# Moving adaLN modulation sums between TensorE and VectorE, and earlier in the program, in a hybrid gMLP / linear-attention layer

## The chip, the cores and the metric

One core of one Trainium2 chip runs the whole layer. The metric is the device time of one execution in microseconds; the median of several runs is given. The kernel is bound by its matrix products, which are all split into three products of 32-bit parts (a high part rounded to fp32r and the rest as a low part: high x high, high x low, low x high).

## The reference

One trunk layer with x (512 tokens, width 2048) and a context (256 tokens). Only x is returned. Six vectors per stream, `mod = silu(c) @ w_mod + b_mod`, modulate the normalised rows; for the context the vector is `c_ctx` and only the first two of the six are needed.

```python
mod_x = split((silu(c) @ w_mod + b_mod), 6);  mod_c = split(silu(c_ctx) @ w_mod + b_mod, 6)
hx = rms_norm(x, g_pre_mix) * (1 + mod_x[1]) + mod_x[0]
hc = rms_norm(xc, g_pre_mix) * (1 + mod_c[1]) + mod_c[0]
ux, vx, qx, kx, vvx, gx, dfx, dbx = split_proj(hx @ w_in)      # the context's likewise, from hc
a_x = spatial_gating(gelu(ux), layer_norm(gelu(vx)))           # gMLP heads
gla_x = bidir_gla(x's q, k, v, decays; states that start from the context's)
x = x + mod_x[2] * rms_norm(concat(a_x, gla_out(gla_x, gx)) @ w_out, g_post_mix)
h2 = rms_norm(x, g_pre_ffn) * (1 + mod_x[4]) + mod_x[3]
x = x + mod_x[5] * rms_norm((silu(h2 @ w1) * (h2 @ w2)) @ w_ffn_out, g_post_ffn)
```

## The kernel before

Activations are held transposed: 16 tiles `hx[k]` of 128 features by 512 tokens for x, 16 tiles `hc[k]` for the context. A tile k of hx needs the modulation of its 128 features, a column of `modA` (gain times 1 + scale) and one of `modB` (shift). `modulated(k)` (L396) turns the tile on TensorE, applies A and B on ScalarE, and makes the high part (ScalarE) and the low part (VectorE).

There are two ways to make the columns. `mod_both(k0)` (L429) makes two tiles for x and context at once on TensorE: the 16 row blocks of `w_mod` are the moving operand, the two conditioning vectors the stationary one, 16 matmuls into two rows of one PSUM bank; then the bias is added on VectorE (L447), eight tiny matmuls (L450) turn the rows into columns, and four VectorE instructions write A and B of both. `mod_ab` (L247) makes nk tiles for one of the two: `mod_acc` (L212) sums over the 16 row blocks on VectorE, one fused multiply-add (L228) of 128 x (2 nk 128) per block, and `mod_ab` then sums over the partitions with 2 nk matmuls of one column each (L257) and writes A and B with two small VectorE instructions (L260, L261). `mod_acc` has a parameter `lag`: how many loads are asked ahead of the multiply-add; `late` in `mod_ab` puts generator steps between the last multiply-add and the column sums.

The order. Everything is issued by one Python program; a list scheduler behind it orders each engine's queue by program order and by when it thinks an operand is ready. Background work is written as generators. In the first products of x (L506 to L542) the loop runs over three groups of tiles, 0 to 3, 4 to 7 and 8 to 15. In each group it does x's keys, the last query head and the decay's low rank together ("k loop", 17 products per tile), then three query heads ("q loop", 9 per tile), then the first half of gMLP's u ("u loop", 12 per tile). After each tile `mods_ahead(2)` takes two steps of the generator `mods_x` (L458): first tiles 2 and 3 by `mod_both(2)`, then x's tiles 4 to 7, 8 to 11 and 12 to 15 by `mod_ab`. Five steps are taken before the loop (L503). `mods_until` forces the steps that a tile needs. Its loads use a pool of ten raw buffers of 512 KB and two accumulators (L419), closed after the u loop of the last group (L543); the context's rows are loaded into the room that it leaves (L570).

Then come the blocks u1, v0 and v1 of the gMLP (16 weight tiles each), the context's keys and values ck and cv, and the linear attention's vv0, vv1, g0, g1. Behind them run two pumps, `bg` and `bgm`, stepped at a rate per weight tile. `bgm` carries the modulation: `ctx_mod` (L550) makes the context's tiles (columns for tiles 4 to 15 in three `mod_ab`, tiles 0 to 3 having come with `mod_both`), at 1.3 steps per weight tile, and is drained after v1 (L662). Then `mods_ffn_in` (L665), the modulation of the FFN norm, at 0.6 in ck and cv and 0.85 in the linear attention (L953), drained at L997. Loads of background sums go to SP's queue by `load_behind` (L198), behind the latest weight load.

Of the kernel before, what the change touches and what calls it, by code (L numbers as in the profile page):

```python
# [18 lines left out]
P = 128  # L19
D = 2048  # L20
KT = D // P
# [71 lines left out]
def trunk_kernel(ctx, tc, cmat, cmask, x, c, ctxt, c_ctx, w_mod, b_mod, g_pre_mix, g_post_mix, g_pre_ffn,  # L93
# [4 lines left out]
    bg, bgm = Pump(), Pump()  # L98
# [11 lines left out]
    def bank(name, main=True):  # L110
        return pm.tile([P, 512], F32, tag="mm" if main else "ms", bufs=6 if main else 2, name=name)
# [4 lines left out]
    def mm(o, l, r, start, stop):  # L116
        return T.matmul(o, lhsT=l, rhs=r, start=start, stop=stop)  # L117
# [20 lines left out]
    cx, cc = cpair[:, :KT], cpair[:, KT:]  # L138
    gpm, gpf, outg, lng = (vec[:, a:b] for a, b in ((0, 16), (16, 32), (32, 40), (40, 48)))
# [54 lines left out]
    def load(dst, src):  # L194

        latest[0] = nc.sync.dma_start(dst, src).ins
# [9 lines left out]
    def mod_pool(pool, nraw, nacc, fetch):  # L206
        return (lambda n: pool.tile([P, 1024], F32, tag="rawm", bufs=nraw, name=n),
                lambda n: pool.tile([P, 1024], F32, tag="macc", bufs=nacc, name=n), fetch)

    mod_bg = mod_pool(stg, 3, 1, load_behind)  # L210
# [33 lines left out]
            yield None  # L244
        yield acc

    def mod_ab(base, k0, nk, cvec, gv, A, B, name, tiles, pin=False, late=0):  # L247

        n = f"{name}{k0}"
        for acc in mod_acc(base + k0 * P, nk * P, 2, cvec, n, tiles, pin):  # L250
            if acc is None:
                yield
        for _ in range(late):
            yield
        ps = bank(n + "ps", False)
        for j in range(2 * nk):
            ins = mm(ps[:, j:j + 1], acc[:, j * P:(j + 1) * P], ones[:, 0:1], True, True)  # L257
            if late and j == 0:
                tc.keep_in_program_order(ins)
        V.tensor_copy(B[:, k0:k0 + nk], ps[:, 0:nk])  # L260
        V.scalar_tensor_tensor(out=A[:, k0:k0 + nk], in0=ps[:, nk:2 * nk], scalar=1.0, in1=gv[:, k0:k0 + nk],  # L261
                               op0=ALU.add, op1=ALU.mult)
        yield
# [99 lines left out]
    cmodA = cp.tile([P, KT], F32, name="cmodA")  # L363
    cmodB = cp.tile([P, KT], F32, name="cmodB")
    fmodA = cp.tile([P, KT], F32, name="fmodA")
    fmodB = cp.tile([P, KT], F32, name="fmodB")
# [52 lines left out]
    mod_first = mod_pool(sp, 10, 2, load_behind)  # L419
# [9 lines left out]
    def mod_both(k0):  # L429

        n = f"mb{k0}"
        ps = bank(n + "ps", False)
        brow = slot(n + "b")[0:2, :]
        for i in range(2):
            nc.scalar.dma_start(brow[:, i * 256:(i + 1) * 256],
                                b_mod[0:1, i * D + k0 * P:i * D + k0 * P + 256].to_broadcast([2, 256]))
        for r0 in range(0, KT, 2):
            raw = mod_first[0](f"{n}w{r0}").rearrange("p (k i c) -> p k i c", k=2, i=2)
            for j in range(2):
                r = r0 + j  # L440
                (load if k0 == 0 else load_behind)(
                    raw[:, j], w_mod[0, r * P:(r + 1) * P, 0:2 * D].rearrange("r (i c) -> r i c", i=2)[
                        :, :, k0 * P:k0 * P + 256])
                mm(ps[0:2, :], cpair[:, r:r + KT + 1:KT], raw[:, j].rearrange("p i c -> p (i c)"), r == 0, r == KT - 1)
            yield
        row = slot(n + "r")[0:2, :]
        V.tensor_tensor(out=row, in0=ps[0:2, :], in1=brow, op=ALU.add)  # L447
        pc = bank(n + "pc", False)
        for j in range(4):
            mm(pc[:, 2 * j:2 * j + 2], row[0:2, j * P:(j + 1) * P], ident[0:2, 0:2], True, True)  # L450
        q = pc[:, 0:8].rearrange("p (i k j) -> p i k j", i=2, k=2)
        k2 = slice(k0, k0 + 2)
        for j, A, B in ((0, modA, modB), (1, cmodA, cmodB)):
            V.tensor_copy(B[:, k2], q[:, 0, :, j])
            V.scalar_tensor_tensor(out=A[:, k2], in0=q[:, 1, :, j], scalar=1.0, in1=gpm[:, k2], op0=ALU.add,
                                   op1=ALU.mult)

    def mods_x():  # L458
        yield from mod_both(2)
        ready[0] = 4  # L460
        yield
        for k0, nk in ((4, 4), (8, 4), (12, 4)):
            yield from mod_ab(0, k0, nk, cx, gpm, modA, modB, "mx", mod_first, k0 == 2)
            ready[0] = k0 + nk
            yield

    ready = [2]
    mx = mods_x()

    def mods_until(k):  # L470
# [3 lines left out]
    def mods_ahead(n):  # L474
        for _ in range(n):
            next(mx, None)
# [23 lines left out]

    for k in range(2):
        first_weights(k)
    mods_ahead(5)  # L503

    upart = [slot(f"up{b}") for b in range(4)]
    for ka, kb in ((0, 4), (4, 8), (8, KT)):  # L506
        first, last = ka == 0, kb == KT
        acc_k = [bank(f"k{h}") for h in range(HB)]
        acc_q = bank("q3")
        acc_d = bank("d")  # L510
        for k in range(ka, kb):
            mods_until(k + 1)
            modulate_until(k + 2)
            first_weights(k)
            wq, wk = w0.pop(k)
            st, sp_ = k == ka, k == kb - 1
            for h in range(HB):
                three(acc_k[h], cut(wk, h * P, P), hx[k], st, sp_)
            three(acc_q, cut(wq, 0, P), hx[k], st, sp_)
            low_rank(acc_d[:64, :], wd[k], hx[k], st, sp_)  # L520
            mods_ahead(2 if k > 1 else 2)
        for h in range(HB):
            land(acc_k[h], kq[h][:, 0, :], first)
        land(acc_q, kq[3][:, 1, :], first, QSCALE)
        land(acc_d, dT[:64, :], first, 1.0, 64)
        accs = [bank(f"q{h}") for h in range(3)]
        for k, (w,) in stream(w_in[0], OQ, 384, kb - ka, f"wq{ka}", k_first=ka):
            for h in range(3):
                three(accs[h], cut(w, h * P, P), hx[ka + k], k == 0, k == kb - ka - 1)
            mods_ahead(2)  # L530
        for h in range(3):
            land(accs[h], kq[h][:, 1, :], first, QSCALE)
        accs = [bank(f"u0{b}") for b in range(4)]
        for k, (w,) in stream(w_in[0], OU, 512, kb - ka, f"wu{ka}", k_first=ka):
            for b in range(4):
                three(accs[b], cut(w, b * P, P), hx[ka + k], k == 0, k == kb - ka - 1)
            mods_ahead(2)
        for b in range(4):
            land(accs[b], upart[b], first)
            if last:  # L540
                S.activation(upart[b], upart[b], AF.Gelu_apprx_tanh)
                nc.scalar.dma_start(u_dr[b], upart[b])  # L542
    sp_ctx.close()  # L543


# [2 lines left out]
    hc = [None] * KT  # L548

    def ctx_mod():  # L550
        for k0 in range(0, KT, 4):
            if k0:
                yield from mod_ab(0, k0, 4, cc, gpm, cmodA, cmodB, "mc", mod_bg, late=2)
            for kb in (k0 // 2, k0 // 2 + 1):
                ps = bank(f"xcp{kb}", False)
                f = slot(f"xcT{kb}")
                for j in range(2):
                    k = 2 * kb + j
                    c = slice(j * CTX, (j + 1) * CTX)
                    turn(ps[:, c], xcn, k)  # L560
                    S.activation(f[:, c], ps[:, c], AF.Identity, bias=cmodB[:, k:k + 1], scale=cmodA[:, k:k + 1])
                hi = hcp.tile([P, 512], F32R, name=f"hch{kb}")
                lo = hcp.tile([P, 512], F32R, name=f"hcl{kb}")
                S.copy(hi, f)
                V.tensor_tensor(out=lo, in0=f, in1=hi.bitcast(F32), op=ALU.subtract)
                for j in range(2):
                    hc[2 * kb + j] = cut((hi, lo), j * CTX, CTX)
                yield

    xcn = [[hcp.tile([P, 512], F32, name=f"xc{t}_{b}") for b in range(4)] for t in range(NC)]  # L570
    for t in range(NC):
        load_rows(xcn[t], ctxt, t)
    normalise(xcn, "xc")[1]()
    bgm.add(ctx_mod())
    bg.rate, bgm.rate = 0.75, 1.3

    def block_ws(w, c0, nb, name, hook=None):
# [77 lines left out]
    for g in range(2):  # L655
# [3 lines left out]
            S.activation(ev, ps, AF.Gelu_apprx_tanh)  # L659
            vt.append(ev)  # L660
        bg.add(gating(g, vt))
    bgm.drain()  # L662


    def mods_ffn_in():  # L665
        for k0 in range(0, KT, 4):
            yield from mod_ab(3 * D, k0, 4, cx, gpf, fmodA, fmodB, "mf", mod_bg, late=1)

    bgm.add(mods_ffn_in())
    bgm.rate = 0.6  # L670
    ckT = [slot(f"ckT{i}") for i in range(2)]
    ckt = [slot(f"ckt{t}") for t in range(NC)]
    cacc = [bank(f"ck{t}") for t in range(NC)]
# [40 lines left out]
    for o in (0, 512):  # L714
        n = min(512, len(LEVELS) * P - o)
        mf = slot(f"mf{o}")
# [233 lines left out]
        bg.add(ctx_state(h))  # L950
    for h in range(HB):
        bg.add(gla_scores(h), 1)
    bg.rate, bgm.rate = 2.4, 0.85  # L953
    for g in range(2):
        for t, ps in enumerate(block_as(w_in[0], OVV + g * 512, f"vv{g}")):
            S.copy(vv[t][g], ps)
# [473 lines left out]
```

## Time and profile before

| | before |
|---|---|
| median of 3 runs | 2330.3 us (2327.45 to 2330.81) |
| the profiled execution | 2326.27 us |
| its span, first to last instruction | 2324.5 us |
| mean granted TensorE clock | 0.99 |
| TensorE / VectorE / ScalarE busy | 97% / 69% / 42% of the span |
| bytes moved | 483.58 MB |

Busy time of TensorE is from the start of one matmul to its modelled end; neighbours overlap, so the pitch of equal matmuls is read from a stretch with their count. The granted clock is 1.00 at 2.4 GHz and 0.50 at 1.2 GHz. The idle time in brackets behind an instruction is that of its engine just before it, and what ended it.

### The profile page before, as it was taken

The page shows a single profiled execution, that of the slowest core. Times are in us where ns is not written, and L with a number is a line of the kernel's source. Part 1 is how long each engine was busy: PE and PEld are TensorE (multiplying, and loading weights), DVE is VectorE, ACT ScalarE, POOL GpSimd, SP SyncE. Part 2 cuts the span into 40 slices and gives each one's busy share as a digit, 9 for nine tenths or more (in the row PEclk, how much of TensorE's full clock was granted, in tenths as well). Part 3 has the DMA queues.
Part 4 walks back from the last instruction along what each step waited for, and adds up shares of the span by engine and source line. Part 5 has one row for each costly group of instructions (what it writes and reads, how often), then busy time and mean ns, then how long its engine had stood idle before and what let it go on. Part 6 is the DMA issues. An engine that isn't in the chain of part 4 may idle for free.

```text
span 2324.5 us, 27744 instructions
## 1 busy us (share of the span) xinstructions
PE 2258.6 (97%) x10298; PEld 1833.0 (79%) x10298; DVE 1599.9 (69%) x2072; ACT 987.6 (42%) x1517; POOL 15.5 (1%) x24
## 2 busy tenths in 40 slices
PE   7999999999999999999999999999999999999998
PEld 2778887788888887777778888888888788888886
DVE  3886587677795656788877877787788643354346
ACT  4444334465565326753333444444445322231232
POOL 0000000000000000000000000000000000000000
PEclk9999999999999999999999999999999999999999
DMA  9966788854452777767776665766575654474344
GB/s 319 329 225 227 246 293 282 274 164 130 152 188 87 261 250 239 231 215 225 235 245 190 217 193 179 226 208 190 177 232 191 221 192 152 133 229 165 120 137 154
DMA packets 255403, 483.58 MB, mean 208 GB/s; under 512 B 21482, under 2 KB 32962, under 8 KB 255268
## 3 DMA queue, kind: packets, MB, share of 16 engines
q1 hardware_dynamic: 243392, 461.98, 61.4%
q10 hardware_dynamic: 11876, 19.84, 2.4%
q8 instruction: 80, 1.31, 0.2%
q14 instruction: 55, 0.45, 0.1%
HBM read 455.52 MB, written 26.22 MB: 207 GB/s over the span
## 4 chain that ended last, share of the span: by engine, by line
PE 82%; DMA 8%; DVE 6%; ACT 2%; issue 1%; SPq 0%; DVEq 0%; ACTq 0%
PE fo L117 16%; PE wo L117 4%; PE f9p L117 3%; PE f5p L117 3%; PE f6p L117 3%; PE f7p L117 3%; PE f8p L117 3%; PE f4p L117 3%; PE f3p L117 3%; PE f10p L117 3%; PE f1p L117 3%; PE f2p L117 2%; PE vv1a L117 2%; PE v0a L117 2%; PE u1a L117 2%; PE k L117 2%
## 5 line engine op out<-in xcount | busy, mean ns | idle before, releaser
L1239 DVE TENSOR_TENSOR gl<-gr,gh 128x512 fp32r<-128x512 f32 x44 | 29.1, 687 | 26.3 <-ACT gh L1238 26.2
L1238 ACT CAST gh<-gr 128x512 fp32r<-128x512 f32 x44 | 25.4, 618 | 48.2 <-DMA gr<-g_dr 41.3
L228 DVE SCALAR_TENSOR_TENSOR m21acc<-m21w,cpair,m21acc 128x1024 f32<-128x1024 f32 x16 | 20.5, 1283 | 15.8 <-DMA m21w<-in_w_mod_dram 15.6
L228 DVE SCALAR_TENSOR_TENSOR m53acc<-m53w,cpair,m53acc 128x512 f32<-128x512 f32 x16 | 12.0, 751 | 27.5 <-DMA m53w<-in_w_mod_dram 27.5
L856 ACT ACTIVATE lv<-lv 128x1024 f32<-128x1024 f32 x20 | 21.0, 1056 | 21.8 <-DVE lv L855 21.8
L117 PE MATMUL fo<-fo_0h,gh 128*128 128x512 f32 x64 | 26.2, 409 | 2.3 <-DVE f10w L1196 2.0
L117 PE MATMUL vv0a<-vv_0h,hxh 128*128 128x512 f32 x64 | 27.4, 431 | 0.0
L117 PE MATMUL g1a<-hxh,g_0h 128*128 128x512 f32 x64 | 27.1, 423 | 0.3 <-ACT g_0h L288 0.3
L228 DVE SCALAR_TENSOR_TENSOR m20acc<-m20w,cpair,m20acc 128x1024 f32<-128x1024 f32 x16 | 20.5, 1283 | 9.8 <-DMA m20w<-in_w_mod_dram 6.6
L1394 ACT ACTIVATE junk<-fc 128x512 bf16<-128x512 f32 x16 | 10.1, 631 | 40.4 <-DVE fc L1393 40.3
L117 PEld LDWEIGHTS s<-lv 128*128 128x128 f32 x192 | 25.0, 191 | 2.5 <-issue 0.5
L117 PE MATMUL g0a<-hxh,g_0h 128*128 128x512 f32 x64 | 26.8, 419 | 0.0
L117 PE MATMUL vv1a<-vv_0h,hxh 128*128 128x512 f32 x64 | 26.4, 427 | 0.0
L117 PE MATMUL g0a<-hxh,g_0l 128*128 128x512 f32 x64 | 25.8, 402 | 0.0
L117 PE MATMUL vv0a<-vv_0l,hxh 128*128 128x512 f32 x64 | 25.7, 402 | 0.0
L117 PE MATMUL fo<-fo_12h,gh 128*128 128x512 f32 x64 | 25.7, 402 | 0.0
L117 PE MATMUL v1a<-v_0h,hxh 128*128 128x512 f32 x64 | 25.7, 402 | 0.0
L117 PE MATMUL s<-lv 128*128 128x128 f32 x192 | 25.6, 275 | 0.1
L117 PE MATMUL vv0a<-vv_0h,hxl 128*128 128x512 f32 x64 | 25.6, 400 | 0.0
L117 PE MATMUL fo<-fo_2l,gh 128*128 128x512 f32 x64 | 25.0, 391 | 0.5 <-DVE fo_2l L1021 0.5
L117 PE MATMUL vv1a<-vv_0l,hxh 128*128 128x512 f32 x64 | 25.4, 398 | 0.0
L117 PE MATMUL fo<-fo_0l,gh 128*128 128x512 f32 x64 | 25.4, 397 | 0.0
(3897 smaller groups left out, 7845.1 us busy)
## 6 DMA issues: line engine op xcount, KB each, us to landing
fo_r<-in_w_ffn_out_dram SPq DMA_DIRECT2D x80, 512.0 KB
gr<-g_dr SPq DMA_DIRECT2D x22, 512.0 KB
mx4w<-in_w_mod_dram SPq DMA_DIRECT2D x16, 512.0 KB
mx8w<-in_w_mod_dram SPq DMA_DIRECT2D x16, 512.0 KB
mx12w<-in_w_mod_dram SPq DMA_DIRECT2D x16, 512.0 KB
mc4w<-in_w_mod_dram SPq DMA_DIRECT2D x16, 512.0 KB
mc8w<-in_w_mod_dram SPq DMA_DIRECT2D x16, 512.0 KB
mc12w<-in_w_mod_dram SPq DMA_DIRECT2D x16, 512.0 KB
```

What stands on the lines that cost most here:

```text
L117: return T.matmul(o, lhsT=l, rhs=r, start=start, stop=stop)
L228: ins = V.scalar_tensor_tensor(out=acc, in0=raw[:, j].rearrange("p i c -> p (i c)"), scalar=cvec[:, k0 + j:k0 + j + 1], in1=acc, op0=ALU.m ...
L856: S.activation(lv, lv, AF.Exp)
L1238: S.copy(hi, r[:, j * 512:(j + 1) * 512])
L1239: V.tensor_tensor(out=lo, in0=r[:, j * 512:(j + 1) * 512], in1=hi.bitcast(F32), op=ALU.subtract)
L1394: S.activation(junk, f, AF.Square, accum_out=fss[:, cg:cg + 1])
```

## The change

It makes x's tiles 2 and 3 by `mod_ab` on VectorE in place of `mod_both(2)` on TensorE. The context's tiles 2 and 3, which `mod_both(2)` made along, and its tiles 4 to 7 are now made by `mod_ab` as further steps of `mods_x`, after x's last ones and still in the loop of x's first products (`AHEAD`); what is left of the generator after the loop is run out before the pool is closed. Eight steps, not five, are taken ahead of the loop. `mods_ffn_in` is added to `bgm` directly behind `ctx_mod`, and the drain after v1 is replaced by running until the context's last tile is there. The background sums take `lag=1`. The rates of `bgm` become 0.8 in ck and cv (0.6 before) and 0.6 in the linear attention (0.85 before).

```diff
-    def mod_ab(base, k0, nk, cvec, gv, A, B, name, tiles, pin=False, late=0):
+    def mod_ab(base, k0, nk, cvec, gv, A, B, name, tiles, pin=False, late=0, lag=0):
 
         n = f"{name}{k0}"
-        for acc in mod_acc(base + k0 * P, nk * P, 2, cvec, n, tiles, pin):
+        for acc in mod_acc(base + k0 * P, nk * P, 2, cvec, n, tiles, pin, lag=lag):
...
-                (load if k0 == 0 else load_behind)(
+                load(
...
     def mods_x():
-        yield from mod_both(2)
-        ready[0] = 4
-        yield
-        for k0, nk in ((4, 4), (8, 4), (12, 4)):
+        for k0, nk in ((2, 2), (4, 4), (8, 4), (12, 4)):
             yield from mod_ab(0, k0, nk, cx, gpm, modA, modB, "mx", mod_first, k0 == 2)
             ready[0] = k0 + nk
             yield
-
+        for k0, nk in AHEAD:
+            yield from mod_ab(0, k0, nk, cc, gpm, cmodA, cmodB, "mc", mod_first, late=2)
+
+    AHEAD = ((2, 2), (4, 4))
...
-    mods_ahead(5)
+    mods_ahead(8)
...
+    for _ in mx:
+        pass
     sp_ctx.close()
...
     def ctx_mod():
-        for k0 in range(0, KT, 4):
-            if k0:
-                yield from mod_ab(0, k0, 4, cc, gpm, cmodA, cmodB, "mc", mod_bg, late=2)
-            for kb in (k0 // 2, k0 // 2 + 1):
+        for k0, nk in ((0, 2), (2, 2), (4, 4), (8, 4), (12, 4)):
+            if k0 and (k0, nk) not in AHEAD:
+                yield from mod_ab(0, k0, nk, cc, gpm, cmodA, cmodB, "mc", mod_bg, late=2, lag=1)
+            for kb in range(k0 // 2, (k0 + nk) // 2):
...
+    def mods_ffn_in():
+        for k0 in range(0, KT, 4):
+            yield from mod_ab(3 * D, k0, 4, cx, gpf, fmodA, fmodB, "mf", mod_bg, late=1, lag=1)
+
...
     bgm.add(ctx_mod())
+    bgm.add(mods_ffn_in())
     bg.rate, bgm.rate = 0.75, 1.3
...
-    bgm.drain()
-
-
-    def mods_ffn_in():
-        for k0 in range(0, KT, 4):
-            yield from mod_ab(3 * D, k0, 4, cx, gpf, fmodA, fmodB, "mf", mod_bg, late=1)
-
-    bgm.add(mods_ffn_in())
-    bgm.rate = 0.6
+    while hc[KT - 1] is None:
+        bgm.run(1)
+
+
+    bgm.rate = 0.8
...
-    bg.rate, bgm.rate = 2.4, 0.85
+    bg.rate, bgm.rate = 2.4, 0.6
```

## Rows read from the trace of the kernel before

**Rows 1.** The page, busy time, share of the span and instructions.
```profile
PE 2258.6 (97%) x10298; PEld 1833.0 (79%) x10298; DVE 1599.9 (69%) x2072; ACT 987.6 (42%) x1517; POOL 15.5 (1%) x24
```

**Rows 2.** Waits of TensorE: us in total, times, longest.
```profile
PE s L117 <- DVE lv L852: 1.9, 1, 1.9
PE ck L117 <- DVE ck_0l L289: 0.7, 1, 0.7
```

**Rows 3.** Stretches: length, each engine's busy us (count), clock, DMA share, GB/s.
```profile
40.46:65.20 24.74, 23.34 (x87) 10.92 (x85) 10.14 (x15) 9.95 (x18) 0.00 (x0) 1.00 1.06 377
65.20:89.40 24.20, 24.20 (x106) 19.76 (x107) 20.98 (x24) 11.22 (x21) 0.00 (x0) 1.00 0.98 348
89.40:122.10 32.70, 32.17 (x155) 25.85 (x154) 29.34 (x39) 13.19 (x24) 0.96 (x1) 1.00 0.87 312
122.10:155.00 32.90, 29.67 (x144) 23.18 (x142) 31.05 (x42) 11.47 (x22) 0.00 (x0) 1.00 0.66 217
155.00:175.30 20.30, 19.98 (x102) 16.01 (x103) 12.27 (x40) 14.24 (x33) 0.00 (x0) 1.00 0.60 194
175.30:191.60 16.30, 16.30 (x73) 13.50 (x72) 7.78 (x17) 8.36 (x15) 0.00 (x0) 1.00 0.46 133
191.60:213.20 21.60, 21.60 (x97) 17.87 (x96) 12.38 (x15) 6.05 (x9) 0.00 (x0) 1.00 0.72 236
```
The engines are PE, PEld, DVE, ACT and POOL, in this order.

**Rows 4.** TensorE's timeline, column sums: start us, us, count [idle before].
```profile
89.42 1.84 PE L117 MATMUL mx4ps<-mats,mx4acc 128*128 128x1 f32 x16
...
154.96 1.92 PE L117 MATMUL mx12ps<-mats,mx12acc 128*128 128x1 f32 x16 [1.37 <-issue]
```

**Rows 5.** TensorE's groups, 30 to 95 us: busy us, mean ns.
```profile
L117 PE MATMUL mb2ps<-mb2w,cpair 128*2 128x512 f32 x32 | 15.1, 624 | 0.0
```

**Rows 6.** TensorE's timeline around tiles 2 and 3.
```profile
61.51 1.05 PE L117 MATMUL mb2pc<-mats,mb2r 2*128 2x2 f32 x8 [0.77 <-DVE mb2r L447]
...
65.17 1.21 PE L117 MATMUL k<-hxh,w0k2h 128*128 128x512 f32 x4 [0.62 <-ACT hxh L403]
```

**Rows 7.** VectorE's timeline: tile 1's low part, and tiles 2 and 3.
```profile
39.77 0.69 DVE L404 TENSOR_TENSOR hxl<-hf,hxh 128x512 fp32r<-128x512 f32 x1 [0.56 <-ACT hxh L403]
...
60.78 0.68 DVE L447 TENSOR_TENSOR mb2r<-mb2ps,mb2b 2x512 f32<-2x512 f32 x1
```

**Rows 8.** VectorE's multiply-adds: two groups, and one stretch of the timeline.
```profile
L228 DVE SCALAR_TENSOR_TENSOR m53acc<-m53w,cpair,m53acc 128x512 f32<-128x512 f32 x16 | 12.0, 751 | 27.5 <-DMA m53w<-in_w_mod_dram 27.5
L228 DVE SCALAR_TENSOR_TENSOR mx4acc<-mx4w,cpair,mx4acc 128x1024 f32<-128x1024 f32 x16 | 20.5, 1282 | 0.2
78.42 5.25 DVE L228 SCALAR_TENSOR_TENSOR mx4acc<-mx4w,cpair,mx4acc 128x1024 f32<-128x1024 f32 x4
```

**Rows 9.** SP's timeline: loads for tiles 2 and 3; the context's rows.
```profile
31.66 10.07 SPq L204 DMA_DIRECT2D mb2w<-in_w_mod_dram  x16
...
156.94 0.33 SPq L196 DMA_DIRECT2D xc<-in_ctx_dram  x1
```

**Rows 10.** Stretches around idle time of TensorE, columns as in rows 3.
```profile
451.90:455.90 4.00, 0.00 (x0) 0.00 (x0) 2.90 (x4) 2.17 (x3) 0.00 (x0) 1.00 0.79 240
455.90:462.70 6.80, 6.71 (x16) 5.13 (x17) 5.61 (x7) 4.67 (x9) 0.00 (x0) 0.50 0.54 155
154.95:161.75 6.80, 6.47 (x40) 5.38 (x41) 2.32 (x7) 3.43 (x7) 0.00 (x0) 1.00 0.52 157
391.00:394.40 3.40, 3.40 (x9) 2.69 (x9) 1.89 (x3) 0.64 (x2) 0.00 (x0) 0.50 0.98 346
```

**Rows 11.** VectorE's timeline in the q loop of tiles 4 to 7.
```profile
114.01 1.27 DVE L228 SCALAR_TENSOR_TENSOR mx8acc<-mx8w,cpair,mx8acc 128x1024 f32<-128x1024 f32 x1
115.20 0.54 DVE L289 TENSOR_TENSOR wq_0l<-wq4r,wq_0h 128x384 fp32r<-128x384 f32 x1
115.67 1.27 DVE L228 SCALAR_TENSOR_TENSOR mx8acc<-mx8w,cpair,mx8acc 128x1024 f32<-128x1024 f32 x1
116.86 0.54 DVE L289 TENSOR_TENSOR wq_0l<-wq4r,wq_0h 128x384 fp32r<-128x384 f32 x1
117.33 2.59 DVE L228 SCALAR_TENSOR_TENSOR mx8acc<-mx8w,cpair,mx8acc 128x1024 f32<-128x1024 f32 x2
```

## The prediction, made before the changed kernel was built

> **What bounds the kernel.** I read the page first, then the waits of TensorE, then the first 213 us in seven stretches, because the change is mostly there, and last the single instructions around tiles 2 and 3. The page says that TensorE is busy for 97% of the span [rows 1]. It is the bound, and the time can only move by work that leaves its queue, by idle time, or by its clock. Its waits are small and scattered [rows 2]. The stretches [rows 3] tell which engine is next. From 40 to 65 us VectorE works 10.1 us of 24.7, so it has room. From 89 to 155 us it works 29.3 of 32.7 and 31.1 of 32.9, so there it is as full as TensorE. The point where the two meet is the modulation of tiles 12 to 15: TensorE waits 1.37 us in front of mx12ps [rows 4].
>
> **Tiles 2 and 3 leave TensorE.** The 32 records of mb2ps, 15.1 us, go [rows 5], and so do the eight mb2pc matmuls of 1.05 us and the 0.77 us wait ahead of them [rows 6]. In their place come eight records of four column sums, half of the 1.84 us that mx4ps takes for sixteen [rows 4], so 0.9 us. That is 15.2 us of work less (15.1 + 1.05 - 0.9), and no gain at this place can be larger than that and the wait together.
>
> What decides is when tile 2 is ready. VectorE has the low part of tile 1 done at 39.77 + 0.69 = 40.46 us [rows 7] and then nothing until tile 2. Into that room come 16 multiply-adds of 128x512. One alone takes 0.751 us, and a chain in which each reads the last one's sum takes 0.04 us more per link (four of the 1282 ns ones took 5.25 us) [rows 8], so 16 x 0.79 = 12.6 us, ending at 53.1. The loads do not hold it: all 16 are issued by 41.7 us [rows 9], and at 377 GB/s [rows 3] a 256 KB load takes 0.7 us, less than one multiply-add. In the kernel before, the row of sums mb2r ended at 60.78 + 0.68 = 61.46 [rows 7] and tile 2's first product began at 65.17 [rows 6], a tail of 3.7 us through TensorE, ScalarE and back. I keep that tail: the first product at 56.8, **8.4 us earlier**. The low parts of tiles 2 and 3 lie in VectorE's queue behind the chain, but before the tail ends.
>
> **The clock gives some of it back.** With mb2ps gone TensorE has 34 products for tiles 0 and 1, 34 x 0.223 = 7.6 us (21.6 us for 97 in the last stretch of [rows 3]), ready to run by 40.5, and then nothing from about 48 to 53. After 4 us without a matmul the granted clock was 0.50, that is 1.2 GHz, for 6.8 us; after the 1.37 us wait at mx12ps it stayed 1.00 [rows 10]. A shorter stretch at 0.50, of 3.4 us, stands at 391 us [rows 10]. So I charge 3.4 to 6.8 us at half speed, 1.7 to 3.4 us lost, and take 2.6: the long one is the nearest row, but part of it can fall into the idle time itself. Net gain at this place 5.8 us.
>
> The Trainium skill, TensorE: Matmul & The Clock Gate, section What's actually happening, speaks against the change here: it says that the throttled clock is the default and only activity releases it, so that matmuls which look like waste keep the others fast. Read strictly, the rule would also charge the small stalls that I allow below with a cold stretch of their own, and the sum would end 1.7 us higher; the row after the 1.37 us wait, at 1.00, does not bear that out.
>
> **VectorE up to tile 12.** From 40.46 to 89.4 it works 10.1 + 21.0 = 31.1 us [rows 3]; with 12.6 more and mb2r's 0.7 less it is 43.0, so it passes that point at 83.5 at the earliest. TensorE comes to mx4ps at 89.4 - 5.8 = 83.6. They arrive together. From there to 155 VectorE is nearly full, moves as one block and holds a lead of this size but no larger one. If it keeps all of its gaps between 65 and 89 (3.2 us [rows 3]) the gain at mx12ps is 3; if the clock costs the least and the chain interleaves with nothing, it is 8. I take 5.8.
>
> **The context's tiles 2 to 7 in x's first products.** TensorE gets one more 0.9 us of column sums (tiles 2 and 3 came free with mb2ps). VectorE gets 16 x 0.79 + 16 x 1.28 = 33 us and the queue of SP 32 more loads, 4.2 MB of them new, between mx12ps and the end of u's first half. In 155 to 213 us VectorE works 12.3 + 7.8 + 12.4 = 32.5 of 58.2 us [rows 3], of which some 6 us are already mc4's first five multiply-adds, so 59 of 58 would be wanted, if all had to be done there; the last of it may trail, and the context's row statistics move out. The loads have room: the DMA share there is 0.46 to 0.72. The tight place is the q loop, 175.3 to 191.6: two steps of the generator per weight tile mean up to 13 multiply-adds, 16 us, and VectorE already works 7.8 us of those 16.3. Up to 7 us of delay, if a weight's low part has to wait for both. The kernel before has the same pattern at 114 to 117 us, and there one or two multiply-adds stand between two low parts while TensorE ran on [rows 11]; the sums trail into the u loop, where VectorE has 9 us. So I take 1.5 us; ends 0 and 7.
>
> Because these sums use the pool that is closed afterwards, the context's rows, loaded at 156.9 before [rows 9], now come some 40 us later. Nobody needs their product until the context's keys, three blocks later (u1, v0, v1), so I cost it at nothing; if ScalarE's scaling of them blocked u1's casts it would be up to 3 us.
>
> **Later stages.** With a third of the context done, and the FFN norm's sums following without a break, the drain after v1 is gone: the 0.7 us wait of ck on VectorE should go. By the rates, the steps of the FFN norm's sums in the linear attention fall from about 54 to 38, some 15 multiply-adds of 1.28 us, and the 1.9 us wait there on lv may go [rows 2]. I take 1.7 in all; ends 0 and 2.6. The context's state and the FFN are otherwise untouched. That is worth little because VectorE was covered there.
>
> **Sum.** -5.8 + 0.9 + 1.5 - 1.7 = -5.1 us. The profiled execution took 2326.27 us (span 2324.5), so 2321.2 in its terms; it lies 4.0 under the median of the three runs, 2330.3, so I predict **2325.2 us**. The bounds are -8 + 0.9 - 2.6 = -9.7 and -3 + 0.9 + 7 + 3 = +8. About 0.2%, 4.7 us, is what a measurement of this kernel can tell from no change.
>
> **Rivals.**
> *The q loop takes it back.* VectorE's queue follows program order strictly and each low part waits for two multiply-adds. For it: VectorE has no lead at mx12ps, so there is no store to live on. Against: [rows 11]. Time: -5.8 + 0.9 + 7 - 1.7 = +0.4, 2330.7.
> *Slower: VectorE becomes the bound of the first products.* From 40.46 to 155 it works 91.5 of 114.5 us [rows 3], 23 us idle; the chain adds 12. Much of that idle time was spent waiting for ScalarE and TensorE. If 16 of the 23 us stay, tile 12 comes at 40.5 + 91.5 + 12 + 16 = 160, 5 us later than now. It decides from 11 us kept. Time: +5 + 0.9 + 1.5 - 1.7 = +5.7, 2336.0. Against it: 10 us of the idle time is one piece, just where the chain goes.
> *All of it.* VectorE's gaps close, the cold stretch falls into the idle time, and TensorE keeps most of its 15.2 us: -12.5 + 0.9 - 1.7 = -13.3, 2317.0. It needs VectorE at 155 - 12.5 with under 1 us idle in all since 40.46, hardly.
> *It does not do what it says.* The products of tile 2 still start at about 65 us, since something else is late (its weight's split, in the same queue): -1.7 + 0.9 + 0.5, no change, 2330.
>
> **Chances.** Forecast (-2 to -9.7) 0.48, of which 0.33 is beyond 4.7 us; q loop 0.20 and no effect 0.06, of which 0.22 is within 0.2% and 0.04 slower; slower by VectorE 0.14; all of it 0.12. Faster 0.45, same 0.37, slower 0.18. The range reaches to the third rival's middle and most of the second: 2315 to 2335.5. The likeliest case alone has 2320.6 to 2328.
>
> **What would show it.** Right: no mb2ps; VectorE in a chain of 16 from 40 to 53 us; tile 2's first product near 57; a clock of 0.5 behind a TensorE gap of 5 us or more; mx12ps near 149; all of v0 begun 4 to 5 us earlier. The sum fails if mx12ps stands at 155 or later, if TensorE shows waits on wq's or wu's low parts in the q and u loops of more than 3 us, or if new waits stand at the start of u1. If the time falls by over 10 us, the chain was faster or the clock held.

## The result, and the profile after

The changed kernel is slower: 2343.55 us against 2329.68 us for the kernel before on the same chip (medians of four runs each). The ratio on record is 1.0053, 95% interval 1.0031 to 1.0075; it is not the quotient of the two medians, which is 1.0060. The time is outside the range of the prediction, on the slow side. The profiled execution took 2345.91 us, span 2344.1 us, so 19.6 us more than the one before, where the medians differ by 13.9; part of what the two traces show is which executions were profiled, and I say below where.

The busy line of the page after, to set beside [rows 1]. TensorE is busy for as long as before, although 15 us of its work left: more of what remains ran at half clock (mean granted clock 0.983, before 0.990).

```profile
PE 2260.6 (96%) x10274; PEld 1839.6 (78%) x10274; DVE 1620.2 (69%) x2103; ACT 987.0 (42%) x1517; POOL 16.5 (1%) x26
```

The same seven stretches as in [rows 3], same columns, in the kernel after. They are cut by time, so that after's work in each is up to 7 us further along before 155 us, and about level with it by 191; what counts is the load on VectorE and on the DMA.

```profile
40.46:65.20 24.74, 17.47 (x77) 14.57 (x77) 22.07 (x32) 12.57 (x23) 0.95 (x1) 0.79 0.98 340
65.20:89.40 24.20, 22.43 (x105) 18.02 (x104) 21.79 (x24) 8.40 (x18) 0.96 (x1) 1.00 1.04 383
89.40:122.10 32.70, 31.55 (x154) 24.75 (x153) 30.84 (x42) 13.33 (x25) 0.53 (x1) 1.00 0.96 346
122.10:155.00 32.90, 30.67 (x148) 23.75 (x147) 31.39 (x45) 11.91 (x23) 0.96 (x1) 0.99 0.81 272
155.00:175.30 20.30, 20.20 (x78) 15.44 (x78) 18.32 (x30) 7.45 (x14) 0.00 (x0) 0.85 0.91 312
175.30:191.60 16.30, 16.30 (x78) 13.58 (x77) 15.18 (x19) 3.20 (x6) 0.00 (x0) 1.00 1.05 386
191.60:213.20 21.60, 18.52 (x89) 14.92 (x88) 13.53 (x19) 6.27 (x14) 0.00 (x0) 1.00 0.57 172
```

From 175.3 to 191.6 us VectorE works 15.18 of 16.30 us (7.78 before), and the DMA share is 1.05 at 386 GB/s (0.46 and 133 before). I had looked at the load before the change and called it room.

Now the lead or lag of the profiled execution after against the one before, at the start or end of TensorE's groups: at mx4ps 6.9 us early, at mx12ps 4.5 early, at the end of the k loop 1.0 early, of the q loop 0.1 early, of the u loop 5.4 late, of u1 14.8, of v1 15.1, at the start of ck 14.3, at its end 19.3, at the start of wo (the product with `w_out`) 15.6, at the end 20.1. The groups overlap a little, so that ck starts before v1 ends. The first gain is there; it is lost between 150 and 275 us, and again around ck.

TensorE's timeline after: first the gap ahead of tile 2, then mx12ps, then the waits in the u loop and in u1.

```profile
53.43 1.84 PE L117 MATMUL mx2ps<-mats,mx2acc 128*128 128x1 f32 x8 [7.27 <-issue]
58.70 1.20 PE L117 MATMUL k<-hxh,w0k2h 128*128 128x512 f32 x4
...
150.53 1.84 PE L117 MATMUL mx12ps<-mats,mx12acc 128*128 128x1 f32 x16
...
196.29 1.20 PE L117 MATMUL u<-hxh,wu_0l 128*128 128x512 f32 x4 [2.99 <-DVE wu_0l L289]
...
203.16 1.84 PE L117 MATMUL mc4ps<-mats,mc4acc 128*128 128x1 f32 x16
...
226.52 0.44 PE L357 MATMUL xcp<-mats,xc 128*128 128x128 f32 x2 [0.40 <-ACT xc L348]
...
230.65 0.89 PE L357 MATMUL xcp<-mats,xc 128*128 128x128 f32 x4 [2.53 <-ACT xcT L563]
...
233.69 0.69 PE L357 MATMUL xcp<-mats,xc 128*128 128x128 f32 x2 [1.05 <-ACT xcT L563]
```

**The u loop, 5.5 us lost.** 1.84 us of it is mc4ps, which stood in v0 before, so that is moved and no loss in itself; 3.0 us is the wait at 196.29. What made it is in the stretches 160 to 206 us, and in the queues of SP, ScalarE and VectorE.

```profile
160.00:175.00 15.00, 15.00 (x67) 11.85 (x66) 13.55 (x23) 5.82 (x11) 0.00 (x0) 0.96 1.01 343
...
193.20:196.30 3.10, 0.11 (x2) 0.01 (x1) 3.10 (x5) 1.14 (x2) 0.00 (x0) 1.00 0.04 15
```

SP's timeline, then ScalarE's, then VectorE's:

```profile
178.88 0.42 SPq L196 DMA_DIRECT2D wu8r<-in_w_in_dram  x1
...
205.08 4.17 SPq L196 DMA_DIRECT2D xc<-in_ctx_dram  x8
```

```profile
187.81 1.14 ACT L288 CAST wu_0h<-wu8r 128x512 fp32r<-128x512 f32 x2 [4.16 <-DMA wu8r<-in_w_in_dram]
...
225.75 0.72 ACT L348 ACTIVATE xc<-xc,xc1r 128x512 f32<-128x512 f32 x1 [3.08 <-DMA u_dr<-up]
...
233.53 0.61 ACT L288 CAST u_0h<-u1r 128x512 fp32r<-128x512 f32 x1
```

```profile
188.56 1.28 DVE L228 SCALAR_TENSOR_TENSOR mc4acc<-mc4w,cpair,mc4acc 128x1024 f32<-128x1024 f32 x1
190.16 0.69 DVE L427 SCALAR_TENSOR_TENSOR kq<-q,kq 128x512 f32<-128x512 f32 x1 [0.33 <-PE q L117]
190.77 1.28 DVE L228 SCALAR_TENSOR_TENSOR mc4acc<-mc4w,cpair,mc4acc 128x1024 f32<-128x1024 f32 x1
191.96 0.68 DVE L427 SCALAR_TENSOR_TENSOR kq<-q,kq 128x512 f32<-128x512 f32 x1
192.56 1.28 DVE L228 SCALAR_TENSOR_TENSOR mc4acc<-mc4w,cpair,mc4acc 128x1024 f32<-128x1024 f32 x1
193.75 0.69 DVE L427 SCALAR_TENSOR_TENSOR kq<-q,kq 128x512 f32<-128x512 f32 x1
194.35 1.28 DVE L228 SCALAR_TENSOR_TENSOR mc4acc<-mc4w,cpair,mc4acc 128x1024 f32<-128x1024 f32 x1
195.55 0.68 DVE L289 TENSOR_TENSOR wu_0l<-wu8r,wu_0h 128x512 fp32r<-128x512 f32 x1
...
225.55 0.16 DVE L186 SCALAR_TENSOR_TENSOR xc1r<-xc1t,xc1r 128x1 f32<-128x1 f32 x1
```

The load with the first two weights of u was issued at 178.88 behind a DMA that had been full since 160 us, and their casts began at 187.81, 8.9 us later. The Trainium skill, DMA: Bandwidth & Descriptors, section Queues, rings and completion order, says that SP owns one ring on each DMA engine and that it is consumed in order; the late landing agrees, though no run here shows the rings themselves. The low part that TensorE waited for is that of the first weight, and it could be made from about 188.4 us, when the first cast had ended. But in VectorE's queue four of the context's multiply-adds and three landings of q (kq, products moved out of PSUM) stood ahead of it, so it came at 195.55, 7 us later. During the wait itself the DMA was idle (0.04) and VectorE full (3.10 of 3.10 us): what ended last was VectorE's queue.

**u1, 9.4 us lost.** The context's rows are read at 205.08 us (156.94 before, [rows 9]). Their chain of small VectorE instructions ends at 225.55, with multiply-adds between its links (the trace puts ScalarE's wait before 225.75 down to a DMA, but xc1r came last). ScalarE then scales the rows, applies the context's modulation, and only at 233.53 casts u1's next weight. TensorE waits 4.2 us in four pieces at the context's transposes. It then runs 6.8 us at half clock, 5.91 of them busy, so some 3.0 us are lost:

```profile
232.80:239.60 6.80, 5.91 (x15) 4.44 (x16) 4.37 (x7) 4.73 (x10) 0.00 (x0) 0.50 0.53 164
```

Eight transposes more than before fall into u1 (16, not 8), some 1.6 us moved from later: 4.2 + 3.0 + 1.6 = 8.8 of the 9.4.

**ck, about 5 us lost.** TensorE's and ScalarE's waits from 372 to 416 us (totals, times, longest):

```profile
PE ck L117 <- ACT ck_0h L288: 4.0, 3, 1.7
PE ck L117 <- DVE ck_0l L289: 1.3, 1, 1.3
```

```profile
ACT ck_0h L288 <- DMA ckr<-in_w_in_dram: 6.2, 4, 4.6
```

### The profile page after: what moved, and what is told of

Its sections match the earlier page's. It is cut to its first block, busy times and chain, and to the rows that moved or that the text cites. A ratio compares the mean times of both kernels' runs of the same rounds, so it can differ in the third digit from the quotient of the medians.

```text
span 2344.1 us, 27768 instructions
## 1 busy us (share of the span) xinstructions
PE 2260.6 (96%) x10274; PEld 1839.6 (78%) x10274; DVE 1620.2 (69%) x2103; ACT 987.0 (42%) x1517; POOL 16.5 (1%) x26
## 4 chain that ended last, share of the span: by engine, by line
PE 76%; DMA 11%; DVE 8%; issue 3%; ACT 3%; SPq 0%; DVEq 0%; POOL 0%; ACTq 0%
PE fo L117 16%; PE f3p L117 3%; PE f8p L117 3%; PE f6p L117 3%; PE f9p L117 3%; PE f7p L117 3%; PE f4p L117 3%; PE wo L117 3%; PE f10p L117 3%; PE f5p L117 3%; PE f1p L117 3%; PE f2p L117 2%; PE vv1a L117 2%; PE g1a L117 2%; PE g0a L117 2%
## 5 line engine op out<-in xcount | busy, mean ns | idle before, releaser
L1241 ACT CAST gh<-gr 128x512 fp32r<-128x512 f32 x44 | 25.5, 618 | 48.4 <-DMA gr<-g_dr 41.5
L860 DVE TENSOR_TENSOR lv<-lv,kq 128x1024 f32<-128x1024 f32 x20 | 24.3, 1221 | 4.7 <-ACT lv L859 4.7
L117 PE MATMUL u<-hxh,wu_0l 128*128 128x512 f32 x64 | 23.4, 399 | 4.1 <-DVE wu_0l L289 4.0
L117 PE MATMUL u<-hxh,wu_0h 128*128 128x512 f32 x64 | 25.6, 400 | 1.2 <-ACT wu_0h L288 1.2
L117 PE MATMUL u1a<-hxh,u_0h 128*128 128x512 f32 x64 | 26.4, 412 | 0.0
L117 PE MATMUL u1a<-hxl,u_0h 128*128 128x512 f32 x64 | 26.0, 406 | 0.0
L228 DVE SCALAR_TENSOR_TENSOR mc12acc<-mc12w,cpair,mc12acc 128x1024 f32<-128x1024 f32 x16 | 20.5, 1283 | 7.7 <-DMA mc12w<-in_w_mod_dram 7.5
```

The source lines that it names most:

```text
L228: ins = V.scalar_tensor_tensor(out=acc, in0=raw[:, j].rearrange("p i c -> p (i c)"), scalar=cvec[:, k0 + j:k0 + j + 1], in1=acc, op0=ALU.m ...
L860: V.tensor_tensor(out=lv, in0=lv, in1=kq[h], op=ALU.mult)
L1241: S.copy(hi, r[:, j * 512:(j + 1) * 512])
```

## The experiments

All ratios are those on record to the kernel before on the same chip, with 95% intervals; lags in us are those of the profiled execution against the one of before, as above. The profiled executions of one code differ by some 2 us at mx12ps already (2.9 to 5.1 us early in the changed kernel and in the runs that change nothing ahead of it), so single lags carry that much. My theory after the result: the change gains at tiles 2 and 3 what I forecast, and loses it and more by the context's sums in the first products, in two ways: they overload DMA and VectorE in the q and u loops, and they hold the pool, so that the context's rows come late. The rivals: the FFN norm's sums in u1 to ck cost it; or VectorE alone, or the transfers alone, are at fault.

### No sums of the context ahead

```diff
-    AHEAD = ((2, 2), (4, 4))
+    AHEAD = ()
...
-    bg.rate, bgm.rate = 0.75, 1.3
+    bg.rate, bgm.rate = 0.75, 1.7
```

> The changed kernel, but no context sums in x's first products (AHEAD is empty); the context's four sums all run in u1 to v1, at 1.7 steps per weight tile instead of 1.3 so that they end with v1. Theory (the context's loads and sums in the first products cost the time: 5.6 us in the u loop behind late weights, 9.4 us at the start of u1 behind late context rows): both go, tiles 2 and 3 on VectorE keep their 4.5 us at mx12ps, so 2326 us (2322 to 2331). Rival (the loss is made by the FFN norm's sums and the new rates in ck): 2338 or more.

2362.85 against 2333.46 us, ratio 1.0126 (1.0104 to 1.0147), far from the theory's 2326. The u loop ends 4.3 us early and u1 starts so: the loss there is gone. But the sums crowd u1 to v1, where the lead of 4.3 turns into a lag of 19.9. TensorE's waits from 200 to 360 us:

```profile
PE mc8ps L117 <- issue: 5.1, 1, 5.1
PE mc4ps L117 <- issue: 3.4, 1, 3.4
```

The rest, to 35.4 us at wo, is the FFN norm's sums, still undone after g1 and drained there. The work has to go somewhere, and this is no better place. So the time of this run doesn't tell the theory from its rival.

### The context's rows read when they are, but used ten steps later

```diff
     def ctx_mod():
+        for _ in range(10):
+            yield
```

> The changed kernel with ten empty steps ahead of the context's tiles, so that TensorE meets the context's first transposes some 20 us later in u1. Theory (at the start of u1 TensorE stands behind the scaling of context rows that came too late): the 4 us of waits at xcp and the 6.8 us stretch at half clock go, 2336 us (2333 to 2339). Rival (it is the transfers and ScalarE's queue that hold u1's weights, whoever waits first): 2341 or more.

2340.83 against 2333.46 us, ratio 1.0033 (1.0020 to 1.0045), just above the theory's 2333 to 2339. u1 loses 1.6 us in place of 9.4, and its stretch at half clock is gone. TensorE's waits from 190 to 275 us are the u loop's and one of 0.3 us:

```profile
PE u L117 <- DVE wu_0l L289: 3.0, 1, 3.0
PE u1a L117 <- ACT u_0h L288: 0.3, 1, 0.3
```

So the transposes of late rows, in TensorE's and ScalarE's queues ahead of u1's work, make most of the loss in u1. Part comes back as 4.2 us in v0 and some 6 us of drained sums ahead of wo.

### Only the context's tiles 2 and 3 ahead

```diff
-    AHEAD = ((2, 2), (4, 4))
+    AHEAD = ((2, 2),)
...
-    bg.rate, bgm.rate = 0.75, 1.3
+    bg.rate, bgm.rate = 0.75, 1.45
```

> The changed kernel with only the context's tiles 2 and 3 summed in x's first products; tiles 4 to 7 go back behind u1, at 1.45 steps per weight tile instead of 1.3. Theory: the 8.4 MB of tiles 4 to 7 are what delays the weights of the u loop and the context's rows, so nearly all of the 15 us comes back: 2328 us (2324 to 2333). Rival (any sums of the context there keep the pool open too long): 2336 or more.

2355.82 against 2333.46 us, ratio 1.0097 (1.0075 to 1.0119), far above the theory's 2324 to 2333. The u loop ends 2.7 us early, so its loss comes with tiles 4 to 7. u1 loses 6.0 us with a wait of 3.9 us on u_0l, v0 6, v1 8, and the drain ahead of wo adds 16.5: at these rates the sums left for later don't fit behind u1 to g1.

### The FFN norm's sums as before

```diff
-            yield from mod_ab(3 * D, k0, 4, cx, gpf, fmodA, fmodB, "mf", mod_bg, late=1, lag=1)
+            yield from mod_ab(3 * D, k0, 4, cx, gpf, fmodA, fmodB, "mf", mod_bg, late=1)
...
     bgm.add(ctx_mod())
-    bgm.add(mods_ffn_in())
...
-    bgm.rate = 0.8
+    bgm.add(mods_ffn_in())
+    bgm.rate = 0.6
...
-    bg.rate, bgm.rate = 2.4, 0.6
+    bg.rate, bgm.rate = 2.4, 0.85
```

> The changed kernel with the FFN norm's sums where and as they were before (added after v1, rates 0.6 and 0.85, no load ahead). Theory: ck gets its 5 us back and the linear attention loses the 4 us that it had gained, 2342.5 us (2340 to 2345). Rival (the 5 us in ck come from the FFN norm's sums, but the gain in the linear attention does not): 2338. Other rival (ck's 5 us have another cause): 2347.

2349.16 against 2333.46 us, ratio 1.0068 (1.0051 to 1.0084). ck loses nothing more (16.6 late at its start, 14.5 at its end), but the linear attention gains nothing either (15.0 at wo; 15.6 in the changed kernel). The 5 us lost in ck and the 4 us regained by wo belong to this part. v1 loses 4.5 us here (0.3 in the changed kernel), with a wait of 2.1 us at the context's transposes and two stretches of 3.4 us at half clock, and whether that belongs to this part or to the one execution isn't shown. By the medians the loss is no smaller without this part, so the rival that it made the loss falls.

### The kernel before with tiles 2 and 3 alone

```diff
-        yield from mod_both(2)
-        ready[0] = 4
-        yield
-        for k0, nk in ((4, 4), (8, 4), (12, 4)):
+        for k0, nk in ((2, 2), (4, 4), (8, 4), (12, 4)):
...
+        for k0, nk in AHEAD:
+            yield from mod_ab(0, k0, nk, cc, gpm, cmodA, cmodB, "mc", mod_first, late=2)
...
+    AHEAD = ((2, 2),)
...
-    mods_ahead(5)
+    mods_ahead(8)
```

> The kernel before with one part of the change: tiles 2 and 3 of x by VectorE, the context's tiles 2 and 3 summed ahead in the last group of x's first products; the context's other sums, the FFN norm's sums and all rates as before. Theory (this part is a gain, the others lose it): 3 to 4.5 us at mx12ps, less 1 in the u loop, less up to 3 in u1 since the context's rows still wait for the pool: ratio to the kernel before 0.998 to 1.000. Rival (the late rows cost more than tiles 2 and 3 give): 1.002 or more.

2330.87 against 2330.56 us, ratio 1.0004 (0.9991 to 1.0016): no difference. mx12ps is 4.8 us early and the u loop ends 3.8 us early, but u1 takes 4.8 us back. At 221.95 us TensorE waits 2.77 us on a low part of u1, and VectorE's timeline shows what it stood behind:

```profile
220.00 1.28 DVE L228 SCALAR_TENSOR_TENSOR mc4acc<-mc4w,cpair,mc4acc 128x1024 f32<-128x1024 f32 x1 [2.47 <-DMA mc4w<-in_w_mod_dram]
221.21 0.68 DVE L289 TENSOR_TENSOR u_0l<-u1r,u_0h 128x512 fp32r<-128x512 f32 x1
```

That is a multiply-add of the context's sums, which itself waited 2.47 us for its load; on the rows' transposes TensorE doesn't wait here.

This run lacks three things of the one before it: the context's tiles 4 to 7 ahead, the loads asked ahead (`lag=1`) for the context's other sums, and the changed end of v1. At 1.0004 and 1.0068 their intervals are far apart, so the loss comes with these three. The traces point to tiles 4 to 7; the other two were not run alone.

### The changed kernel with the context's rows early

```diff
+    xcq = xc_ctx.enter_context(tc.tile_pool(name="xcq", bufs=1))
...
-    mod_first = mod_pool(sp, 10, 2, load_behind)
+    mod_first = mod_pool(sp, 6, 2, load_behind)
...
+        if last:
+            for t in range(NC):
+                load_rows(xcn[t], ctxt, t)
+            normalise(xcn, "xc")[1]()
```

> The changed kernel with the context's rows in a pool of their own, loaded and normalised after the k loop of the last group (room for it: six raw buffers for the first sums instead of ten). Theory (u1 loses 9 us because the rows wait for the pool): u1 loses at most 2 us, ratio to the kernel before 1.0015 to 1.003 (the changed kernel: 1.0053). Rival (u1's loss is ScalarE's and VectorE's queue order, whenever the rows come): 1.005. If six raw buffers are too few, mx12ps comes later than 151 us and that is told apart by the profile.

2341.42 against 2330.56 us, ratio 1.0054 (1.0035 to 1.0074), as slow as the change. u1 loses 1.2 us in place of 9.4, as the theory has it; but the u loop now ends 11.3 us late. TensorE's waits from 175 to 245 us:

```profile
PE u L117 <- DVE wu_0l L289: 1.7, 1, 1.7
PE u L117 <- ACT wu_0h L288: 1.6, 1, 1.6
PE q L117 <- DVE wq_0l L289: 1.1, 2, 0.6
PE q L117 <- ACT wq_0h L288: 0.8, 1, 0.8
```

The cost moved to the q and u loops, where the rows' loads and squares now stand. I read it as a stage with more work than it holds, in which late rows were only where part of it showed; but the run also has six raw buffers in place of ten, and what they cost isn't separated. mx12ps came at 151.6 us, past the 151 of the sign for too few buffers; the run with a quarter of the loads, which has ten, has 151.6 as well.

### A quarter of the context's loads, a quarter of its sums

Two halves of one question, in tiles 4 to 7 of the context alone: 128x256 of each raw block are loaded but summed at full size, or all is loaded and 128x256 summed.

```diff
+                if quarter == "load":
+                    o, r = acc.rearrange("p (n c) -> p n c", c=256), raw[:, j, 0, 0:256].unsqueeze(1).to_broadcast([P, 4, 256])
+                elif quarter == "sum":
+                    o, r = acc[:, 0:256], r[:, 0:256]
```

> The changed kernel, but of the context's tiles 4 to 7 only a quarter of each weight row block is loaded (2.1 instead of 8.4 MB) and read four times, so that VectorE's work stays and the transfers go; the output is not the reference's. Theory (the u loop waits for weights that queue behind those loads): the wait of 3 us at wu's low part and the low DMA share behind it go, the u loop ends 4 to 5 us earlier, and the rows too. Rival (VectorE's 16 multiply-adds of 1.28 us hold the low parts): no change there.

> The changed kernel, but the multiply-adds of the context's tiles 4 to 7 take 256 of the 1024 columns, so that the transfers stay and three quarters of 20 us of VectorE work go; the output is not the reference's. Theory (transfers): the wait at wu's low part stays within 1 us. Rival (VectorE): it goes.

Loads: 2343.37 against 2330.56 us, ratio 1.0060 (1.0040 to 1.0080). Sums: 2340.29 against the same, ratio 1.0042 (1.0022 to 1.0062). With a quarter of the loads the u loop has no wait and ends 0.9 us late in place of 5.4; with a quarter of the sums it has one of 1.1 us and ends 2.0 late. Either removal gives back most of it, so the wait needed both, and neither rival stands alone.

How the loads act is seen in VectorE's queue. With a quarter of them the program issues the same instructions in the same order, and yet two low parts of u now stand ahead of the q loop's landings, which come before them in the changed kernel (L298 and L436 are that kernel's L289 and L427):

```profile
186.26 0.68 DVE L298 TENSOR_TENSOR wu_0l<-wu8r,wu_0h 128x512 fp32r<-128x512 f32 x1
...
188.06 0.68 DVE L298 TENSOR_TENSOR wu_0l<-wu8r,wu_0h 128x512 fp32r<-128x512 f32 x1
...
189.85 0.68 DVE L436 SCALAR_TENSOR_TENSOR kq<-q,kq 128x512 f32<-128x512 f32 x1
```

So the loads moved the low part's place in the queue, most likely by when the scheduler thought that the weight would land; that was not shown. The landing itself was not what ended last: with the rows used later the first cast came at 190.00, 2.2 us later than in the changed kernel, and the wait was 3.0 us as well.

Neither run is faster than the change by its interval. Both still lose in u1, 12.0 and 8.5 us, since the rows are late as before. TensorE's waits from 175 to 275 us with a quarter of the loads:

```profile
PE xcp L366 <- ACT xcT L572: 3.7, 1, 3.7
PE u1a L117 <- DVE u_0l L298: 1.9, 1, 1.9
```

### Tiles 2 and 3 alone, with the context's rows early

The last two runs build on the kernel before with tiles 2 and 3 alone: it has the gain and not the overload, and loses in u1 only. The rows get buffers of their own as above, and are read after the last group's k loop, or its q loop.

> The kernel before with tiles 2 and 3 of x by VectorE and only the context's tiles 2 and 3 ahead (the run before of that kind came out at 2330.9 us, ratio 1.0004: 4.8 us early at the end of the x sums, 3.8 us early at the end of the u loop, then 4.8 us lost in u1), and the context's rows in their own buffers, read and normalised right after the last group's k loop; the raw buffers of the first products go from ten to six for it. Theory (the loss in u1 comes from rows that wait for the pool of the first products): u1 loses at most 1.5 us instead of 4.8, and some 2 to 4 us of the lead reach the end of the program: 2326 to 2329 us, ratio 0.998 to 0.999. Rival (the stage is overcommitted, and the loss moves to wherever there is room to lose): the rows' loads and squares in the q loop, or the four raw buffers fewer, cost the q and u loops what u1 gives back: the end of u1 within 1 us of that of the kernel before, 2330 to 2333 us.

> The same as the run beside it, with the context's rows read and normalised one loop later, after the last group's q loop, about where the kernel before reads them (156.9 us). Theory of late rows: as good as the run beside it in u1, at most 1.5 us lost there; 2326 to 2329 us. Rival (overcommitted stage): the same 2330 to 2333 us, with the loss in the u loop instead of the q loop.

After the k loop: 2328.64 against 2331.60 us, ratio 0.9986 (0.9974 to 0.9998). After the q loop: 2327.96 us against the same, ratio 0.9979 (0.9965 to 0.9993). Both are faster than the kernel before by little, in time as the theory had it, and both keep u1: in the second it takes 44.5 us, with no wait of TensorE in it (the window is u1, columns as in [rows 3]; and SP's timeline).

```profile
211.70:256.20 44.50, 44.50 (x202) 36.75 (x201) 27.91 (x34) 16.67 (x29) 0.00 (x0) 1.00 0.83 282
```

```profile
165.59 3.81 SPq L196 DMA_DIRECT2D xc<-in_ctx_dram  x8
```

With the rows after the k loop there is a wait of 1.1 us on wq_0l in the q loop, and of the 4.1 us lead at mx12ps 1.4 are left at the end of the q loop: there the rival was partly right. At wo the leads are 3.7 and 1.7 us. The two are not told apart by their intervals. They also have six raw buffers, not ten, so that what the buffers cost or gain by themselves isn't separated. And as u1's loss in the run that they build on was a wait on VectorE's queue and not on the rows, by which way the early rows remove it isn't shown.

## Why the prediction was wrong

**Tiles 2 and 3: right in mechanism, and nearly in size.** The chain of multiply-adds ended at 53.3 us (forecast 53.1), and TensorE waited 7.27 us. That the end fits to 0.2 us is partly luck: one of the 16 ran ahead of tile 1's low part, at 39.22, and a longer one of the next sum stood before the last. VectorE's timeline after:

```profile
40.49 10.98 DVE L228 SCALAR_TENSOR_TENSOR mx2acc<-mx2w,cpair,mx2acc 128x512 f32<-128x512 f32 x14
51.38 1.28 DVE L228 SCALAR_TENSOR_TENSOR mx4acc<-mx4w,cpair,mx4acc 128x1024 f32<-128x1024 f32 x1
52.58 0.75 DVE L228 SCALAR_TENSOR_TENSOR mx2acc<-mx2w,cpair,mx2acc 128x512 f32<-128x512 f32 x1
```

The granted clock was 0.50 from 48.4 to 58.7 us (the 0.79 of the first stretch), of which 5.3 us are not idle. The tail from the end of the chain to tile 2's first product took 5.4 us in place of the 3.7 that I kept, so 1.7 us were lost there, the least of the forecast 1.7 to 3.4 (I took 2.6). That product began at 58.7, 6.5 us earlier than before. At mx12ps 4.5 us were gained, and 4.8 with this part alone, for a forecast of 5.8 between 3 and 8.

**The first step that failed: "the loads have room: the DMA share there is 0.46 to 0.72", and with it the 1.5 us for the q and u loops.** I counted the 32 loads, but not their bytes against the time in which they would run: 4.2 MB new and 8.4 MB brought forward are 12.6 MB, at the 377 GB/s of [rows 3] 33 us of the DMA. They did not spread over the 58 us from 155 to 213, where the share rose only from 0.61 to 0.82 on average (from the stretches above and [rows 3]). They ran in its first part: the share is 1.01 to 1.05 from 160 to 191 us and 0.57 after, and u's first weights could be cast only at 187.81. I priced the two loops by VectorE's pattern in [rows 11], one or two multiply-adds between two low parts; in the u loop four multiply-adds and three landings stood ahead of the first low part, which came 7 us after its weight's cast. The two loops cost 6.5 us in place of 0.9 + 1.5, of which 2.7 are column sums. The q loop, which I called the tight place, lost no more than its column sums, 0.9 us; the u loop, where I had counted on room of VectorE, lost 5.5. The run with a quarter of the loads shows the transfers' part, the one with a quarter of the sums VectorE's.

**The second: the context's rows, "at nothing ... up to 3 us".** The mechanism of the 3 us, ScalarE's scaling ahead of u1's casts, was part of what came, but the reason for the zero was wrong. Nobody needs the rows before ck, yet the engines take their queues in order, and the first transposes stand among u1's products. TensorE waited for them, and the wait brought cold clock. u1 lost 9.4 us, 1.6 of which is moved work; using the rows ten steps later cut it to 1.6.

**The third: later stages, -1.7.** From the end of u1 to wo the lag went from 14.8 to 15.6, with 5 us lost in ck to weight loads behind the FFN's sums, and 4 regained. The run with the FFN's sums as before comes to about the same net, 13.9 to 15.0, with its loss in v1 instead.

**The rest of the profile's 20 us** lies in single executions. After mx12ps the clock fell to 0.50 from 154.3 to 161.1 us, and the k loop lost 3.5 us; the run with the rows used later has the same code up to there, kept 1.00 in that place and lost 1.5. From wo to the end the lag grows from 15.6 to 20.1, with two cold stretches of 6.8 us, at 953 and 1035 us, where the profiled kernel before had 3.4 each. No kernel here changes anything from wo on, and yet the lag moves there by -1.7 us (no sums of the context ahead) to +10.2 (tiles 2 and 3 alone, rows after the k loop), so these 4.5 us say nothing of the change. The profiles differ by 5.8 us more than the medians, and I take it that most of that lies in these two places; that they come out otherwise in the median execution was not shown.

**The rivals.** "The q loop takes it back" had VectorE's half of the mechanism, at 7 us and no more, but the loss came one loop later, in the u loop. The slower rival put VectorE's limit ahead of mx12ps, where it did not show. Of the signs that I named for a wrong sum two came: waits on wq's and wu's low parts, 4.5 us in the three groups of tiles (2.99 of them in the last u loop; none are listed before), and new waits at the start of u1. mx12ps at 155 us or later did not come.

## What to carry to other kernels

Before moving background work into a stage, add its bytes and its engine time, moved ones included, to what the stage already has: a DMA share of 0.46 is no room for loads that all come at once, and an engine that takes its queue in order and has no slack passes every delay on. Look also at what the moved work holds, here a pool whose release starts other loads, and at where the instructions that use those loads stand in the queues; that place, not the final use, is their due time. A good part of a change can be lost in the company of a bad one: tiles 2 and 3 alone, with the rows kept early, are faster than the kernel before, by 0.1 to 0.2%.

## What the runs showed of the hardware

How long a stall lasts was no guide to whether the clock falls. TensorE's stretches right after a stall: in the kernel after, behind 2.99 us without a matmul, then behind two gaps of 0.32 and 0.30 us; then, in the kernel before with tiles 2 and 3 alone, behind 2.77 us (1.35 us after its end).

```profile
196.30:203.10 6.80, 6.72 (x28) 5.22 (x29) 6.62 (x8) 1.25 (x2) 0.00 (x0) 1.00 0.31 83
...
154.30:161.10 6.80, 6.40 (x15) 4.51 (x15) 5.52 (x10) 3.14 (x6) 0.00 (x0) 0.50 0.73 244
```

```profile
223.30:226.70 3.40, 3.40 (x10) 2.63 (x9) 2.30 (x4) 0.62 (x1) 0.00 (x0) 0.50 0.92 317
```

The longest of the three left the clock at 1.00, and the shorter two were followed by 0.50, that is 1.2 GHz. Ahead of the fall at 154.3 us TensorE had run 16 one-column sums and 12 transposes of 128x128 from 150.53 on. The code alone doesn't decide it: in the same place the run with the FFN norm's sums as before had 3.4 us at 0.50 (from 153.1), and the one with the rows used later had none. The Trainium skill, TensorE: Matmul & The Clock Gate, section What's actually happening, says that the throttled clock is the default. I had set that rule aside after one row at 1.00; the two stretches where the granted clock fell agree with it, and the one at 1.00 shows that not every stall is followed by a cold stretch. So a cold stretch of the lengths seen belongs in the range for each new stall, not in the sum.
